# Six temporary tiles, a later load of the rope factors and later tails of products in a four-layer hybrid block

## The chip, the cores and the metric

The kernel runs on one core of one Trainium2 chip. The metric is the device time of one execution in microseconds (us). Before the change the median of three runs is 2697.6 us (2693.47 to 2699.81).

## The reference

A sequence of 1024 tokens (1024 wide) gets 16 learned tokens ahead of it, 1040 in all, and passes four layers. Each adds a branch of its normalised input to the residual:

```python
for i in range(DEPTH):
    kind = i % N_MIXERS
    j = i // N_MIXERS
    u = rmsnorm(h, norm_gain[i])
    if kind == 0:
        y = attention_branch(u, a_w_in[j], a_q_gain[j], a_k_gain[j], a_sinks[j], a_w_out[j], valid, pos)
    elif kind == 1:
        y = mlstm_branch(u, b_w_in[j], b_conv_w[j], b_conv_b[j], b_gate_bias[j], b_h_gain[j], b_w_out[j], valid)
    else:
        y = hgrn2_branch(u, c_w_in[j], lower_bounds[i], c_o_gain[j], c_w_out[j], valid)
    h = h + jnp.where(valid[None, :, None], y.astype(h.dtype), 0.0).astype(h.dtype)
```

Layers 1 and 4 are sliding-window attention: q and k are projected, normalised per head by their mean square, rotated (rope), and used in blocks of 128. Layer 2 is an mLSTM. Layer 3 is HGRN2, a linear recurrence with a decay for each key channel:

```python
q, k, v, z = _split(u @ w_in, (A_W, A_KVW, A_KVW, A_W))
q = rope(rmsnorm(q.reshape(bsz, lp, A_HEADS, A_HD), q_gain), pos)
k = rope(rmsnorm(k.reshape(bsz, lp, A_KV, A_HD), k_gain), pos)
...
o = o_inter + jnp.einsum('bhts,bhse->bhte', att, v_)
S_new = jnp.exp(A_last)[..., None] * S + jnp.einsum('bhsd,bhse->bhde', k_ * jnp.exp(A_last[:, :, None] - A), v_)
```

## The kernel before, in words

Everything is held transposed, channels on partitions and tokens along the free dimension, in three chunks of tokens: 0 with 400, 1 with 384, 2 with 256 columns (the last layer's first chunk has 384). Each projection of 1024 inputs to 128 outputs (`proj`, lines 245 to 269) is, for one chunk, 24 matmuls (L262): eight pieces of the inputs, and for each three products of split operands (high by high, high by low, low by high). The weights come by DMA on SP's queue (L240, two halves of 256 KB each) and are split by ScalarE (ACT, L195) and VectorE (DVE, L196).

The order on TensorE (PE) is the program's own: the layers build lists of steps, each with an assumed cost in ns, and `weave`, `later` and `spread` merge them (lines 56 to 108). On ACT, DVE, GpSimd (POOL) and SP a scheduler sets the order from those steps when the program is built, and an order once set is fixed: an instruction that waits holds up what stands behind it on its engine.

**Temporary tiles.** `tmp()` (L139) gives one of TMPS = 5 buffers of 404 columns. They serve the squares of the norms, the normalised input before it is split, the sigmoids, and the q and k chunks. `vtile()` (L136) gives one of 10 tiles that otherwise hold blocks of v.

**A chunk of q or k** (`qk_proj`, L515 to L546) goes like this. `evac`, right behind the chunk's last matmul: the rope factors of its columns are loaded into the one buffer `cs` (L520), ACT copies the product out (L523, tile dst) and squares it (L524, tile sq), and four DMAs copy dst with its halves swapped into the tile rot (L527). `stat`, 2000 ns of steps later: a matmul on PE (L533) sums sq over the partitions of each head, and ACT makes the reciprocal root of it (L361, L362). `rope`, 4000 ns after the chunk: DVE multiplies by the factors (L538 dst, L539 rot), adds (L540) and multiplies by the root (L541). At 6000 ns the chunk is split into high and low parts (`q_split` L492 and L493, `k_split` L473 to L476), and only then dst is free. Three tiles of a chunk are temporaries, except for the first k projection, which has rows of its own. There are 60 such chunks, 30 in layer 1 and 30 in layer 4. By the addresses in the built program, five buffers come to this in a run of q chunks: the Square of a chunk takes the buffer that dst of the chunk two before it held, and rot takes that of rot of the chunk before.

**The norm** (`Norm`, L371 to L425): the squares of eight pieces of x (L377) are summed by DVE (L381) in the tile of the first square, a matmul with ones sums over partitions (L389), and the tile then holds the factor until the eight `unit`s of the chunk have used it (L415).

**Layer 3** (`layer_c`, L1006 to L1283): for each of 8 heads the tokens are worked on in five regions (16, then four of 256). For a region, DVE and ACT make eight tiles X (`level`, L1098), and PE multiplies them in a burst of small matmuls (L1127, L1137). `tail0` (L1144) masks and reduces these products on DVE (L1154, L1163), and POOL copies the result into the tile `att` (L1165). `tail1` transposes keys on PE (L1187). `tail2`, for each block of 128: att times v (L1202), the running state S times the queries (L1204), and the product for the next state (L1209), which DVE adds to S (L1214). S is handed on 64 times, from block to block. The tails of region r are woven with the levels and the burst of region r + 1, behind a step without work that counts as TAIL_LAG = 600 ns:

```python
mx += weave(main[r], last)
last = [[TAIL_LAG, lambda: None, None]] + tails[r]
```

Of the kernel before, what the change touches and what calls it, by code (L numbers as in the profile page):

```python
# [9 lines left out]
F32 = mybir.dt.float32  # L10
# [5 lines left out]
P = 128  # L16
# [18 lines left out]
C_W = 256  # L35
B_COLS = 96
LOOKAHEAD = 12000.0
TAIL_LAG = 600.0
PRIO = 40
ROWS, TMPS, RAWS, YS = 8, 5, 2, 3  # L40
XS = 14
GAP, BURST = 200.0, 1300.0
KT_LAG = 500.0
# [12 lines left out]
def weave(a, b):  # L56

    ta, tb = sum(x[0] for x in a) + 1e-9, sum(x[0] for x in b) + 1e-9
    out, i, j, ca, cb = [], 0, 0, 0.0, 0.0
    while i < len(a) or j < len(b):  # L60
        if j >= len(b) or (i < len(a) and ca / ta <= cb / tb):
            ca += a[i][0]
            out.append(a[i])
            i += 1
        else:
            cb += b[j][0]
            out.append(b[j])
            j += 1
    return out
# [42 lines left out]
def hybrid_kernel(ctx: ExitStack, tc: tile.TileContext, ins, out, layers=(0, 1, 2, 3)):  # L112
    nc = tc.nc
    v, s, g, pe, sp = nc.vector, nc.scalar, nc.gpsimd, nc.tensor, nc.sync
# [11 lines left out]
    def nm(x):  # L126
        ctr[0] += 1
        return f"{x}{ctr[0]}"
# [7 lines left out]
    def vtile():  # L136
        return rpool.tile([P, 258], F32, tag="v", name=nm("v"), bufs=10)

    def tmp():  # L139
        return tpool.tile([P, 404], F32, tag="t", name=nm("t"), bufs=TMPS)  # L140
# [10 lines left out]
    def psa():  # L151
        return psum("pa", 1)
# [92 lines left out]
    def proj(src, evac, chunks=CHUNKS):  # L245
        st = {}

        def pre():
            st["w"] = weights(src, "m")

        groups = []
        for n, (c0, cn) in enumerate(chunks):
            grp = []
            for part in range(4):
                def fn(n=n, c0=c0, cn=cn, part=part):
                    if part == 0:
                        st[n] = psj()
                    h, l = st["w"]
                    acc = st[n]
                    for k in (2 * part, 2 * part + 1):  # L260
                        for i, (a, b) in enumerate(((h, uh), (h, ul), (l, uh))):
                            pe.matmul(acc[:, :cn], a[:, k, :], b[:, k, c0 : c0 + cn],  # L262
                                      start=(k == 0 and i == 0), stop=(k == KT - 1 and i == 2))
                    if part == 3:
                        evac(acc, n, c0, cn)

                grp.append([6 * cn * MM, fn, pre if (n == 0 and part == 0) else None])
            groups.append(grp)
        return groups
# [90 lines left out]
    def rstd_from(acc, dst, cn, n):  # L360
        s.activation(dst[:, :cn], acc[:, :cn], AF.Ln, bias=eps, scale=1.0 / n)  # L361
        s.activation(dst[:, :cn], dst[:, :cn], AF.Exp, scale=-0.5)  # L362
# [8 lines left out]
    class Norm:  # L371
# [1 line left out]
            self.i, self.acc, self.ps = i, {}, {}  # L373

        def sq(self, m, n, c0, cn, size=KT):
            q = tmp()[:, :cn]
            s.activation(q, x[:, m, c0 : c0 + cn], AF.Square)  # L377
            if m % size == 0:
                self.acc[n] = q
            else:  # L380
                v.tensor_tensor(self.acc[n], self.acc[n], q, op=ALU.add)  # L381
# [63 lines left out]
    def layer_a(i, j, first, last, fin):  # L445
        win, wout = ins["a_win"][j], ins["a_wout"][j]
        chunks = LAST_CHUNKS if last else CHUNKS
        R = {}
# [66 lines left out]
        def qk_proj(src, gcol, work, fsplit, ch):  # L515
            late = {}

            def evac(acc, n, c0, cn):
                cos_sin = R["mix"].tile([P, 2, 400], F32, tag="cs", name=nm("cs"), bufs=1)
                sp.dma_start(cos_sin[:, :, :cn], ins["rope"][:, :, c0 : c0 + cn].rearrange("a p t -> p a t"))  # L520
                dst, sq, rot = work(n, c0, cn)
                late[n] = dst, sq, rot, cos_sin
                s.activation(dst, acc[:, :cn], AF.Identity, scale=R["cons"][:, gcol : gcol + 1])  # L523
                s.activation(sq, acc[:, :cn], AF.Square)  # L524
                for q in range(4):
                    o = q ^ 1
                    sp.dma_start(rot[32 * q : 32 * q + 32], dst[32 * o : 32 * o + 32])  # L527

            def finish(n, c0, cn):
                def stat():  # L530
                    dst, sq, rot, _ = late[n]
                    st = psa()
                    pe.matmul(st[:, :cn], R["masks"][:, 0:P], sq, start=True, stop=True)  # L533
                    rstd_from(st, sq, cn, 64)

                def rope():
                    dst, sq, rot, cos_sin = late[n]
                    v.tensor_tensor(dst, dst, cos_sin[:, 0, :cn], op=ALU.mult)  # L538
                    v.tensor_tensor(rot, rot, cos_sin[:, 1, :cn], op=ALU.mult)  # L539
                    v.tensor_tensor(dst, dst, rot, op=ALU.add)  # L540
                    v.tensor_tensor(dst, dst, sq, op=ALU.mult)  # L541

                return [(D_Q[0], [4 * cn * MM, stat, None]), (D_Q[1], [0.0, rope, None]),
                        (D_Q[2], fsplit(lambda: late[n][0], n, c0, cn))]

            return proj(src, evac, ch), [finish(n, *c) for n, c in enumerate(ch)]  # L546

        def tile_of(groups, events):
# [198 lines left out]
        for i in range(3, 12):  # L747
            for t in (2 * (i // 3), 2 * (i // 3) + 1):
                at = [id(z) for z in body]
                q, k = (at.index(id(z)) if id(z) in at else -1  # L750
                        for z in (order["q", t, i % 3], order["S", i // 3 - 1, i % 3]))
# [254 lines left out]
    def layer_c(i, j, fin):  # L1006
# [256 lines left out]
        for h in range(8):  # L1263
# [14 lines left out]
            for r in range(5):  # L1278
                mx += weave(main[r], last)
                last = [[TAIL_LAG, lambda: None, None]] + tails[r]  # L1280
            body += weave(mx, fill)
# [182 lines left out]
```

## Time and profile before

| | us |
|---|---|
| median of 3 runs | 2697.6 |
| the profiled execution | 2690.46 |
| its span, first to last instruction | 2688.7 |
| PE busy | 2590.5 |
| DVE busy | 1959.5 |
| ACT busy | 1693.4 |
| POOL busy | 370.1 |

By the times of the trace, layer 1 runs to about 536 us, layer 2 from there to about 1600, layer 3 to about 2200, and layer 4 to the end. In the profile's rows, "PE pa L533 <- ACT t L524: 37.3, 15, 4.8" reads: PE's matmul of line 533 waited for ACT's instruction of line 524, 37.3 us in total, 15 times, 4.8 us the longest. In a timeline a row is start, duration, engine, line, operation and tiles, and in brackets how long the engine had stood idle and for whom. PEclk is the clock that TensorE was granted, 1.00 being full. SPq is SP's queue, which only issues DMAs.

### The profile page before, as it was taken

To read this page: it belongs to the slowest core of one execution; us is meant where nothing else is said; L and a number is where in the kernel's file an instruction comes from. 1 tells how busy PE (TensorE), PEld (TensorE's weight loads), DVE (VectorE), ACT (ScalarE), POOL (GpSimd) and SP (SyncE) were. 2 spreads that over 40 slices of the span, in tenths; PEclk is the share of its full clock that TensorE was granted. 3 is DMA by queue.
4 is the path that set the end of the run, shared out by engine and by line. 5 is a ranking of instruction groups with operands and counts; after the bars stand their busy time and mean duration, and the time that the engine had idled before them with its cause. 6 is when DMAs were issued, how large, how long until landed. Compare 5 with 4: busy or idle time off the path is not lost.

```text
span 2688.7 us, 54502 instructions
## 1 busy us (share of the span) xinstructions
PE 2590.5 (96%) x20276; PEld 2492.4 (93%) x20276; DVE 1959.5 (73%) x5337; ACT 1693.4 (63%) x4339; POOL 370.1 (14%) x760
## 2 busy tenths in 40 slices
PE   6899999999999999999999999999999998998999
PEld 5898989999999999999999998999999898898999
DVE  7787687974646474747475688978878978886886
ACT  7776777565454545454545657877676857766772
POOL 0343243000000000000000000101000000541450
PEclk8999999999999999999999999999999999999999
DMA  4223111011111111111111111101111013212212
GB/s 148 84 59 96 52 58 46 21 65 56 40 56 40 56 40 56 40 56 40 56 40 53 51 34 33 34 33 34 41 33 39 31 45 107 69 53 88 73 36 75
DMA packets 89786, 145.66 MB, mean 54 GB/s; under 512 B 12448, under 2 KB 42272, under 8 KB 89520
## 3 DMA queue, kind: packets, MB, share of 16 engines
q1 hardware_dynamic: 89520, 142.17, 16.9%
q8 instruction: 160, 2.62, 0.4%
q14 instruction: 106, 0.87, 0.1%
HBM read 127.28 MB, written 4.26 MB: 49 GB/s over the span
## 4 chain that ended last, share of the span: by engine, by line
PE 72%; DVE 12%; ACT 8%; issue 3%; POOL 2%; DMA 2%; SPq 0%; ACTq 0%; DVEq 0%; POOLq 0%
PE pj L262 35%; PE pj L345 14%; PE pj L307 9%; ACT Sm L633 1%; PE po L667 1%; PE pt L648 1%; PE po L890 1%; POOL Sm L637 1%; PE pa L904 1%; PE po L892 1%; DVE t L415 1%; DVE ul L196 1%; DVE Sm L630 1%; DVE x L348 1%; PE pj L303 1%
## 5 line engine op out<-in xcount | busy, mean ns | idle before, releaser
L262 PE MATMUL pj<-uh,wh 128*128 128x256 f32 (+2 forms) x2688 | 930.5, 346 | 3.4 <-ACT uh L195 3.4
L262 PE MATMUL pj<-ul,wh 128*128 128x256 f32 (+2 forms) x2688 | 871.7, 324 | 3.2 <-DVE ul L196 3.1
L262 PE MATMUL pj<-uh,wl 128*128 128x256 f32 (+2 forms) x2688 | 869.6, 324 | 0.0
L262 PEld LDWEIGHTS pj<-uh,wh 128*128 128x128 f32 x2688 | 513.4, 191 | 24.3 <-issue 6.4
L262 PEld LDWEIGHTS pj<-ul,wh 128*128 128x128 f32 x2688 | 513.7, 191 | 15.2 <-DVE ul L196 5.3
L262 PEld LDWEIGHTS pj<-uh,wl 128*128 128x128 f32 x2688 | 513.2, 191 | 0.1
L637 POOL TENSOR_SCALAR Sm<-Sm,s 128x256 f32<-128x256 f32 (+2 forms) x272 | 254.5, 947 | 410.7 <-DVE s L635 406.0
L196 DVE TENSOR_TENSOR wl<-wr,wh 128x512 fp32r<-128x512 f32 x336 | 228.7, 690 | 54.1 <-ACT wh L195 51.8
L195 ACT CAST wh<-wr 128x512 fp32r<-128x512 f32 x336 | 201.9, 616 | 97.9 <-PE pj L345 27.1
L348 DVE TENSOR_TENSOR x<-x,pj 128x384 f32<-128x384 f32 (+2 forms) x480 | 234.7, 510 | 38.8 <-PE pj L345 37.1
L345 PE MATMUL pj<-yh,wh 128*128 128x384 f32 (+2 forms) x768 | 252.9, 329 | 0.0
L345 PE MATMUL pj<-yl,wh 128*128 128x384 f32 (+2 forms) x768 | 248.0, 323 | 3.3 <-DVE yl L196 3.3
L345 PE MATMUL pj<-yh,wl 128*128 128x384 f32 (+2 forms) x768 | 246.6, 321 | 0.0
L307 PE MATMUL pj<-wh,uh 128*128 128x256 f32 x768 | 231.0, 301 | 0.0
L307 PE MATMUL pj<-wh,ul 128*128 128x256 f32 x768 | 216.4, 282 | 0.0
L307 PE MATMUL pj<-wl,uh 128*128 128x256 f32 x768 | 216.1, 281 | 0.0
L633 ACT ACTIVATE Sm<-Sm,s 128x257 f32<-128x257 f32 (+2 forms) x272 | 130.6, 482 | 84.6 <-DVE s L630 75.5
L432 DVE SCALAR_TENSOR_TENSOR t<-pj,t 128x384 f32<-128x384 f32 (+2 forms) x192 | 99.0, 515 | 107.0 <-ACT t L431 106.5
L433 ACT ACTIVATE t<-t 128x384 f32<-128x384 f32 (+2 forms) x240 | 117.8, 491 | 80.1 <-DVE t L432 79.0
L345 PEld LDWEIGHTS pj<-yl,wh 128*128 128x128 f32 x768 | 145.1, 189 | 5.7 <-DVE yl L196 5.2
L195 ACT CAST yh<-r 128x384 fp32r<-128x384 f32 (+2 forms) x120 | 57.3, 479 | 143.8 <-PE pj L345 126.2
L345 PEld LDWEIGHTS pj<-yh,wh 128*128 128x128 f32 x768 | 145.3, 189 | 1.7 <-DVE S L1214 0.3
(235 smaller groups left out, 5470.9 us busy)
## 6 DMA issues: line engine op xcount, KB each, us to landing
wr<-in_b_win SPq DMA_DIRECT2D x128, 256.0 KB, 2.9
wr<-in_a_win SPq DMA_DIRECT2D x80, 256.0 KB, 2.9
wr<-in_c_win SPq DMA_DIRECT2D x64, 256.0 KB, 2.8
cs<-in_rope SPq DMA_DIRECT2D x28, 384.0 KB, 3.3
wr<-in_a_wout SPq DMA_DIRECT2D x32, 256.0 KB, 2.7
wr<-in_b_wout SPq DMA_DIRECT2D x32, 256.0 KB, 2.7
cs<-in_rope SPq DMA_DIRECT2D x20, 256.0 KB, 2.7
t<-t SPq DMA_DIRECT2D x104, 48.0 KB, 2.2
```

What stands on the lines that cost most here:

```text
L195: s.copy(h, src)
L196: v.tensor_tensor(l, src, h.bitcast(F32), op=ALU.subtract)
L262: pe.matmul(acc[:, :cn], a[:, k, :], b[:, k, c0 : c0 + cn], start=(k == 0 and i == 0), stop=(k == KT - 1 and i == 2))
L303: pe.matmul(acc[:48, :256], um[0][:, k, :], m[:, kk, :], start=(k == 0 and m is wh), stop=(k == KT - 1 and m is wl))
L307: pe.matmul(acc[:cn, :256], a[:, k, c0 : c0 + cn], m[:, kk, :], start=(k == 0 and i == 0), stop=(k == KT - 1 and i == 2))
L345: pe.matmul(acc[:, :cn], a[:, k, mc], b, start=(k == 0 and i == 0), stop=(k == 1 and i == 2))
L348: v.tensor_tensor(x[:, m, c0 : c0 + cn], x[:, m, c0 : c0 + cn], acc[:, :cn], op=ALU.add)
L415: v.scalar_tensor_tensor(u, x[:, k, cs], ngain[:, self.i, k : k + 1], self.acc[n], op0=ALU.mult, op1=ALU.mult)
L432: v.scalar_tensor_tensor(a[:, :cn], z, 0.0, a[:, :cn], op0=ALU.min, op1=ALU.subtract)
L433: s.activation(a[:, :cn], a[:, :cn], AF.Exp)
L633: s.activation(Sm[:nq, u, : nk + 1], Sm[:nq, u, : nk + 1], AF.Exp, scale=-1.0, bias=st[:nq, u : u + 1], accum_out=den[:nq, u : u + 1])
L637: g.tensor_scalar(Sm[:nq, u, :nk], Sm[:nq, u, :nk], den[:nq, u : u + 1], None, op0=ALU.mult)
```

## The change

Four things change. TMPS is 6. The first square of a norm sum goes to a tile of the v pool where the chunk is chunk 2, so that this sum holds no temporary; its arithmetic is the same. The load of the rope factors moves from `evac` to `stat`, 2000 ns of steps later, and so behind the four rot DMAs of the same chunk in the program's text. TAIL_LAG is 2000. No instruction is added or taken away; PE's order changes only in layer 3.

```diff
-TAIL_LAG = 600.0
+TAIL_LAG = 2000.0
...
-ROWS, TMPS, RAWS, YS = 8, 5, 2, 3
+ROWS, TMPS, RAWS, YS = 8, 6, 2, 3
...
         def sq(self, m, n, c0, cn, size=KT):
-            q = tmp()[:, :cn]
+            q = (vtile() if n == 2 and m % size == 0 else tmp())[:, :cn]
             s.activation(q, x[:, m, c0 : c0 + cn], AF.Square)
...
             def evac(acc, n, c0, cn):
-                cos_sin = R["mix"].tile([P, 2, 400], F32, tag="cs", name=nm("cs"), bufs=1)
-                sp.dma_start(cos_sin[:, :, :cn], ins["rope"][:, :, c0 : c0 + cn].rearrange("a p t -> p a t"))
                 dst, sq, rot = work(n, c0, cn)
-                late[n] = dst, sq, rot, cos_sin
+                late[n] = dst, sq, rot
...
                 def stat():
-                    dst, sq, rot, _ = late[n]
+                    dst, sq, rot = late[n]
+                    cos_sin = R["mix"].tile([P, 2, 400], F32, tag="cs", name=nm("cs"), bufs=1)
+                    sp.dma_start(cos_sin[:, :, :cn], ins["rope"][:, :, c0 : c0 + cn].rearrange("a p t -> p a t"))
+                    late[n] = dst, sq, rot, cos_sin
```

In the changed program the lines between 521 and 527 stand two earlier (evac is L521 and L522, the rot DMAs L525), the load of the factors is L531, and the lines from 533 on stand one later. By its addresses, six buffers are two sets of three in a run of q chunks: the Square takes the buffer that the Square of the chunk two before it held (last used by the final product of its rope), dst that of rot, and rot that of dst.

**SP's queue, layer 1, the last five chunks of q and k ahead of the second pair's attention (253 to 272 us in the trace of before).** cs is the load of rope factors, `t<-t` a chunk's rot DMAs, wr a weight load. Before:

```order
L520 DMA cs_3084<-in_rope 128x2x256
L527 DMA t_3088<-t_3086 32x256 x4
L240 DMA wr_3437<-in_a_win 128x512
L520 DMA cs_3158<-in_rope 128x2x400
L527 DMA t_3162<-t_3160 32x400 x4
L240 DMA wr_3690<-in_a_win 128x512
L240 DMA wr_3694<-in_a_win 128x512
L520 DMA cs_3214<-in_rope 128x2x384
L527 DMA t_3218<-t_3216 32x384 x4
L520 DMA cs_3254<-in_rope 128x2x256
L527 DMA t_3258<-t_3256 32x256 x4
```

Now, for the same chunks:

```order
L531 DMA cs_3140<-in_rope 128x2x256
L240 DMA wr_3433<-in_a_win 128x512
L525 DMA t_3084<-t_3082 32x256 x4
L240 DMA wr_3437<-in_a_win 128x512
L525 DMA t_3160<-t_3158 32x400 x4
L531 DMA cs_3202<-in_rope 128x2x400
L525 DMA t_3216<-t_3214 32x384 x4
L531 DMA cs_3261<-in_rope 128x2x384
L240 DMA wr_3690<-in_a_win 128x512
L240 DMA wr_3694<-in_a_win 128x512
L531 DMA cs_3306<-in_rope 128x2x256
L525 DMA t_3254<-t_3252 32x256 x4
```

For the 400 and the 384 column chunks the rot DMAs now stand ahead of the chunk's own factors; for the two of 256 the factors still stand first.

**ACT, the last of these chunks (256 columns of k; 267 to 271 us in the trace).** Its copy out (L523) and its Square (L524), with the split of an earlier chunk (L473 to L476) around them. Before:

```order
L523 ACTIVATE t_3256<-pj_3225,cons_194 128x256
L474 CAST r_3279<-t_3160 64x400
L476 CAST r_3280<-r_3280 64x400
L473 CAST r_3281<-t_3160 64x400
L474 CAST r_3281<-t_3160 64x400
L524 ACTIVATE t_3257<-pj_3225 128x256
```

Now:

```order
L362 ACTIVATE t_3215<-t_3215 128x384
L521 ACTIVATE t_3252<-pj_3223,cons_194 128x256
L522 ACTIVATE t_3253<-pj_3223 128x256
L473 CAST r_3277<-t_3158 64x400
L474 CAST r_3277<-t_3158 64x400
```

The Square stood behind the split of the chunk two before it, whose tile it took; it now stands right behind the copy, ahead of that split.

**PE, layer 3, first head, third region (1680 to 1686 us in the trace).** po is the output that tail2 adds up, pa the product for the next state, pm the burst, pj a projection. Before:

```order
L1202 MATMUL po_19376<-att_18665,v_18868 128x128
L1204 MATMUL po_19376<-X_19617,S_19597 128x128
L1209 MATMUL pa_19714<-v_18868,kT_19681 128x128
L262 MATMUL pj_19673<-uh,wh_19440 128x400
L262 MATMUL pj_19673<-ul,wh_19440 128x400
L262 MATMUL pj_19673<-uh,wl_19441 128x400
```

Now:

```order
L262 MATMUL pj_19658<-uh,wl_19447 128x400
L1203 MATMUL po_19376<-att_18665,v_18868 128x128
L1205 MATMUL po_19376<-X_19617,S_19603 128x128
L1210 MATMUL pa_19792<-v_18868,kT_19705 128x128
L1203 MATMUL po_19796<-att_18665,v_18952 128x128
L1205 MATMUL po_19796<-X_19617,S_19794 128x128
L1210 MATMUL pa_19799<-v_18952,kT_19705 128x128
```

Before, six rows of projection, the burst of the next region and six more rows stood between the two blocks of the region. Now the burst stands ahead of both (right behind tail1), and the second block follows the first at once.

## The prediction

> **What bounds the kernel now.** First the page's table of engines and the view of the cores, to see which engine sets the time.
>
> ```profile
> PE 2590.5 (96%) x20276; PEld 2492.4 (93%) x20276; DVE 1959.5 (73%) x5337; ACT 1693.4 (63%) x4339; POOL 370.1 (14%) x760
> core 0: 2688.7 us, clock 0.986
> ```
>
> PE is busy 2590.5 of 2688.7 us. No matmul is added or taken away, so two things can be won: the 2688.7 − 2590.5 = 98.2 us in which PE stands, and the time lost at a lower clock, about 0.014 × 2688.7 = 38 us. Next, where these lie: busy time by layer (start and end, length; PE, PEld, DVE, ACT, POOL with their counts; granted clock, DMA share, GB/s).
>
> ```profile
> 78.00:536.00 458.00, 432.42 (x2825) 414.74 (x2824) 366.79 (x992) 315.40 (x845) 155.56 (x298) 0.98 0.19 57
> 536.00:1600.00 1064.00, 1059.87 (x6973) 1028.61 (x6973) 652.98 (x1647) 561.31 (x1313) 7.68 (x67) 1.00 0.15 48
> 1600.00:2200.00 600.00, 583.30 (x7211) 557.53 (x7210) 500.28 (x1600) 435.61 (x1227) 56.55 (x133) 0.99 0.12 38
> 2200.00:2689.00 489.00, 459.59 (x3018) 444.80 (x3016) 381.87 (x985) 323.42 (x835) 148.56 (x253) 0.98 0.23 69
> ```
>
> Layer 2 is full (4 us idle, clock 1.00): nothing can come from there. The attention layers have 25.6 and 29.4 us idle, layer 3 has 16.7. Third, the view of the waits, which says for whom (total, count, longest).
>
> ```profile
> PE pa L533 <- ACT t L524: 37.3, 15, 4.8
> PE po L1202 <- POOL att L1165: 16.0, 10, 3.5
> PE pa L389 <- DVE t L381: 7.4, 3, 4.0
> PE pt L648 <- POOL Sm L637: 7.3, 14, 1.2
> PE pa L533 <- ACT r L524: 2.1, 1, 2.1
> DVE S L1214 <- PE pa L1209: 15.1, 12, 2.8
> ```
>
> The statistics matmul waits for the Square (L524): 37.3 + 2.1 = 39.4 us, two fifths of all idle time. The attention part of layer 3 waits 16.0 us for `att`. The change touches both.
>
> **Why the Square is late.** SP's and DVE's timelines around 265 us, the place of the longest such wait.
>
> ```profile
> 253.21 0.38 SPq L520 DMA_DIRECT2D cs<-in_rope  x1
> 259.34 0.38 SPq L520 DMA_DIRECT2D cs<-in_rope  x1
> 265.90 0.38 SPq L520 DMA_DIRECT2D cs<-in_rope  x1
> 271.62 0.39 SPq L520 DMA_DIRECT2D cs<-in_rope  x1
> ...
> 258.89 0.42 DVE L539 TENSOR_TENSOR t<-t,cs 128x256 f32<-128x256 f32 x1
> 265.31 0.57 DVE L539 TENSOR_TENSOR t<-t,cs 128x400 f32<-128x400 f32 x1
> 266.51 0.57 DVE L541 TENSOR_TENSOR t<-t,t 128x400 f32<-128x400 f32 x1
> 269.56 0.57 DVE L475 TENSOR_TENSOR r<-t,r 64x400 fp32r<-64x400 f32 x1 [1.31 <-ACT r L473]
> ```
>
> Then ACT's and PE's timelines of the chunk behind.
>
> ```profile
> 267.56 0.47 ACT L523 ACTIVATE t<-pj,cons 128x256 f32<-128x256 f32 x1
> 270.21 0.38 ACT L524 ACTIVATE t<-pj 128x256 f32<-128x256 f32 x1
> 270.65 1.22 PE L533 MATMUL pa<-t,masks 128*128 128x256 f32 x2 [4.77 <-ACT t L524]
> ```
>
> Two things follow one another here. The loads of the factors come 6.13, 6.56 and 5.72 us apart: each starts when the rope before has read the one buffer (258.89 + 0.42, then 259.34; 265.31 + 0.57, then 265.90), and the rot DMAs of its chunk stand behind it on SP. So load, rot and rope form a loop. And the copy out ended at 268.03, but the Square began at 270.21, when the split of the chunk two before (L475, from 269.56) had let go of its tile. PE waited 4.77 us.
>
> **Square waits (term 1).** With six buffers the Square needs only the final product (L541) of the chunk two before: here 266.51 + 0.57 = 267.08. The copy, which by the old rule took the tile that this same product frees (it began at 267.56), needs only L539 of the chunk two before, 265.88, and so stands no longer in the way. The Square moves from 270.21 to 267.08, and 3.1 of the 4.77 us go. The first and last of the eleven long waits (39.4 us with five short ones):
>
> ```profile
> 79.10 0.57 DVE L541 TENSOR_TENSOR t<-t,t 128x400 f32<-128x400 f32 x1
> 81.82 0.38 ACT L524 ACTIVATE t<-pj 128x256 f32<-128x256 f32 x1 [0.69 <-DVE qs L493]
> 82.26 1.22 PE L533 MATMUL pa<-t,masks 128*128 128x256 f32 x2 [3.90 <-ACT t L524]
> ...
> 2538.95 0.56 DVE L541 TENSOR_TENSOR t<-t,t 128x384 f32<-128x384 f32 x1
> 2544.67 1.11 PE L533 MATMUL pa<-t,masks 128*128 128x256 f32 x2 [2.42 <-ACT t L524]
> ```
>
> At 82.26 the Square moves from 81.82 to 79.67, so 2.1 of 3.90 us go; at 2544.67 the product ended at 2539.51, long before PE came, and all of 2.42 goes. Done so for the eleven, with the ropes as late as now, it gives 2.1, 2.2, 1.7, 3.1, 3.8, 0, 2.0, 1.6, 2.3, 3.1 and 2.4, together 24.3. That is the low end; the high end is 39.4. The ropes themselves come sooner where loads follow closely, because the rot DMAs no longer stand behind the load.
>
> ```profile
> DMA to landing us min/median/max: 2.6/3.2/4.5
> ```
>
> The loop is then the load alone and two multiplications: 3.2 + 0.57 + 0.57 = 4.3 us, with hand-overs perhaps 4.7 (estimate), against some 6.1 now. PE needs 24 rows of projection for a chunk, by the chain of waits
>
> ```profile
> 644.96 18.46 PE pj L262 x120
> ```
>
> 18.46 / 120 = 0.154 us each, so 3.7 us: the loop stays the slower of the two, but by 1 us a chunk, not 2.4. I take **30**, two fifths of the way from 24.3 to 39.4. On ACT the splits that stood ahead of the Square now stand behind it; their readers are the attention blocks of the pair, and none of the large waits above is for them.
>
> **Clock behind the waits (term 2).** By the windows, the attention layers lose 0.02 × 458 = 9.2 and 0.02 × 489 = 9.8 us to the clock, and layer 3 loses 0.01 × 600 = 6 (rounding: ±0.005). Where it is lost, two windows and a wait:
>
> ```profile
> 271.00:275.00 4.00, 4.00 (x13) 3.78 (x13) 2.81 (x6) 2.92 (x7) 0.00 (x0) 0.50 0.32 90
> ...
> 1690.95 0.49 PE L1202 MATMUL po<-att,v 128*128 128x128 f32 x2 [2.28 <-POOL att L1165]
> 1691.00:1695.00 4.00, 4.00 (x62) 3.56 (x64) 2.22 (x12) 1.48 (x7) 0.00 (x0) 0.57 0.06 13
> ```
>
> After the wait of 4.77 us PE runs 4 us at half speed; after one of 2.28 us it does so too (0.57). So a wait must be shortened to below 2.28 us at the least to win this back. Of 19 in the attention layers, 30/39.4 is 14.5; as some waits are left near that, I take **12** (8 to 17).
>
> [...]
>
> **Norm sum (term 3).** Chunk 2's sum held one of the five buffers through a chunk of units.
>
> ```profile
> 44.05 1.22 PE L389 MATMUL pa<-t,const 128*128 128x256 f32 x2 [4.05 <-DVE t L381]
> ```
>
> This wait, 4.05 us, is of that chunk. Its squares can start earlier, but the eight sums on DVE still follow one another: 0 to 5, I take **2**. The v tile it takes costs nothing: ten stand there, and at these places the v blocks of the layer are not yet made.
>
> **Layer 3 (term 4).** A step of 2000 ns in place of 600 puts PE work between a region's burst and its tail2. Counted in rows of PE's order times 0.154 us, that distance is 4.9 to 13.4 us before and 9.6 to 19.7 now. The wait for `att` is 3.5 us at the longest, so I take **15** of 16.0 (12 to 16), and **5** of the clock's 6 (3 to 6).
>
> **The new cost (term 5).** What was spread between the blocks of a tail now stands ahead of them, so blocks follow each other more closely, and S is handed on from one to the next: L1209, then DVE's L1214, then the next block. Of the 64 hand-overs, 8 had at most 12 rows of projection between them, and none under 6. Now 4 have none, 15 have six, 11 have nine to thirteen. The shortest and longest hand-over of before:
>
> ```profile
> 2046.43 0.39 PE L1209 MATMUL pa<-v,kT 128*128 128x128 f32 x2
> 2046.85 0.35 DVE L1214 SCALAR_TENSOR_TENSOR S<-S,s,pa 128x128 f32<-128x128 f32 x1
> ...
> 2088.30 0.39 PE L1209 MATMUL pa<-v,kT 128*128 128x128 f32 x2
> 2091.64 0.33 DVE L1214 SCALAR_TENSOR_TENSOR S<-S,s,pa 128x128 f32<-128x128 f32 x1
> ```
>
> They take 0.77 and 3.67 us. Cover is att times v of the next block (0.49 us, row at 1690.95) and the rows, six being 0.92. At 0.77 only the four bare ones wait: 4 × 0.28 = 1 us. Midway, at 2.2 us, 4 × 1.7 + 15 × 0.8 = 19. In the first region, where tail1 now stands right ahead of tail2, PE waits about 1 us more for the transposed keys (estimate, from the same hand-over). I take **−6** of 2 to 20: the quoted short pair is of the close kind, and the long one comes where DVE had other work queued ahead and PE plenty to do.
>
> **Mixers (term 6).** Attention blocks wait 7.3 us for POOL (L648). With the projections done sooner POOL has less head start: 0 to 7 more, I take **−4**.
>
> **Sum.** 30 + 12 + 2 + 15 + 5 − 6 − 4 = 54, against the profiled execution's 2690.46: 2636.5. The median of the runs is 7.1 above that execution, so the forecast is **2643.6**.
>
> **Rivals.**
>
> A, *the later load makes the rope later.* Where the buffer is already free, the load now starts up to 2000 ns of steps later, and the Square waits for L541 of the chunk two before. With ropes 1 us later, each of the eleven gains shrinks by 1: 24.3 becomes 14, the clock gives 6. For it: the landing takes 3.2 us, not hidden if it starts with the statistics. Against: at the places that wait now the loads are held by the buffer, not by the program. 14 + 6 + 2 + 15 + 5 − 6 − 4 = 32: 2658.5, as median 2665.6. Chance 0.17.
>
> B, *hand-overs of S eat layer 3's gain.* Term 5 at its end of 20, and gaps that keep the clock low: 30 + 12 + 2 + 15 − 20 − 4 = 35, median 2662.6. For it: DVE is busy 500 of 600 us there. Chance 0.12.
>
> [...] Chance 0.03.
>
> D, *slower:* DVE stands queued at every close hand-over, each taking the longest 3.67 us. Waits: 4 × 3.2 + 15 × 2.3 + 11 × 1.3 = 61; behind 19 of them 4 us at 0.57, a loss of 1.7 each, 33. Against 30 + 12 + 2 + 15 − 4 = 55 won that is +39: median 2736.6. It decides from a cost of 55, or 1.8 us at each of 30. DVE's L1214 waited for PE in 12 cases and 15.1 us, so DVE is often the one that stands ready; that speaks against. Chance 0.05.
>
> E, *the change moves waits only:* the Square is free, but ACT or the rot DMAs are next, and PE reaches the end as late as now. Nothing is won beyond 0.2%, about 5.4 us, which is what a measurement of this kernel can tell from no change. Against: at 267.08 all that the Square needs is ready. Chance 0.05.
>
> **How the numbers follow.** The forecast has 0.58. All low ends together would be 24 + 8 + 0 + 12 + 3 − 20 − 7 = 20 won (median 2677.6), all high ends 39 + 17 + 5 + 16 + 6 − 2 = 81 (2616.6); neither meets wholly. 2618 to 2676 holds the forecast, A, B and C, and leaves out D, E and the corners. Faster: 0.58 + 0.17 + 0.12 + 0.03 = 0.90; same 0.05; slower 0.05.
>
> **What would show it.** Right: the row of PE waiting for ACT's Square falls from 39 to about 10 us, that for `att` to near nothing; the attention windows show clock 0.99 or 1.00; layer 2 still takes 1064 us; in layer 3 a new wait of PE for L1215's S of a few us. Loads of the factors in close runs come under 5 us apart. Wrong: Square waits of over 20 us (A), waits for S of over 15 us (B, D), or a new long wait on the path in the attention heads (E).

## The result, and the profile after

The changed kernel takes 2652.9 us (median of 4 runs, 2651.9 to 2654.3) against 2698.0 us before (4 runs, 2693.5 to 2699.8). The ratio is 0.9836, with a 95% interval of 0.9819 to 0.9853: 45 us faster. The forecast was 2643.6, 54 us faster, with a range of 2618 to 2676. The profiled execution took 2653.2 us; its span is 37.6 us shorter than that of before. The other 8 us are scatter: the execution profiled before lay some 7.6 us below its median, the one profiled after lies on it.

The page's table of engines and the view of the cores, after:

```profile
PE 2579.2 (97%) x20276; PEld 2481.9 (94%) x20276; DVE 1956.4 (74%) x5337; ACT 1691.1 (64%) x4339; POOL 367.6 (14%) x760
core 0: 2651.1 us, clock 0.992
```

PE's idle time fell from 98.2 to 2651.1 − 2579.2 = 71.9 us, that is by 26.3; its busy time fell by 11.3 for the same 20276 matmuls, and most of that is the clock: by the trace's own records of the granted clock, PE was busy at half clock for 66.1 us before and for 40.0 us after, and half of the difference is 13.0. Together 26.3 and 11.3 are the 37.6.

By layer, with the ends of the stretches moved by as much as the same instructions have moved there:

```profile
77.00:523.00 446.00, 431.13 (x2833) 412.43 (x2833) 369.10 (x998) 316.78 (x851) 155.16 (x297) 0.99 0.20 60
523.00:1586.00 1063.00, 1058.88 (x6984) 1028.12 (x6983) 653.51 (x1648) 563.12 (x1317) 8.06 (x68) 1.00 0.15 48
1586.00:2176.00 590.00, 579.29 (x7211) 556.27 (x7210) 497.55 (x1599) 434.66 (x1227) 55.99 (x133) 0.99 0.12 39
2176.00:2651.00 475.00, 455.22 (x3016) 439.25 (x3015) 382.32 (x984) 323.08 (x834) 146.64 (x253) 0.99 0.24 71
```

Layer 2 stays as it was (1063 us for 1064). Layer 1 takes 12 us less, layer 3 takes 10 and layer 4 takes 14. In the view of PE's waits (total, count, longest) the two large rows have shrunk, and four rows have come or grown (dots stand for rows left out):

```profile
PE pa L534 <- ACT t L522: 12.2, 10, 2.9
...
PE pj L345 <- DVE yl L196: 8.2, 9, 2.8
PE pt L649 <- POOL Sm L638: 7.2, 11, 1.6
PE po L1205 <- DVE S L1215: 5.5, 11, 1.4
...
PE pa L389 <- DVE t L381: 3.5, 2, 3.1
...
PE pm L1138 <- DVE X L1115: 2.5, 1, 2.5
PE pa L389 <- DVE v L381: 2.3, 1, 2.3
PE pa L1210 <- ACT kT L1190: 1.3, 1, 1.3
...
PE po L1203 <- POOL att L1166: 0.6, 1, 0.6
...
PE pa L534 <- ACT r L522: 0.4, 1, 0.4
```

The Square (12.2 + 0.4) costs 12.6 us where it cost 39.4, `att` 0.6 where it cost 16.0. New are the waits for S, for one tile X and for the transposed keys, 9.3 us together, and the output projection's wait for `yl`, which was 3.3 us, is now 8.2. Rows of one kernel scatter between executions: in a second execution of the changed kernel (the mark among the experiments) the Square's two rows are 14.5 + 0.4.

At the place shown before, the loads of the rope factors and the rot DMAs on SP, then the chunk behind on ACT and PE, now read:

```profile
253.57 0.53 SPq L531 DMA_DIRECT2D cs<-in_rope  x1
254.96 2.41 SPq L525 DMA_DIRECT2D t<-t  x4
258.05 0.38 SPq L531 DMA_DIRECT2D cs<-in_rope  x1
263.16 0.38 SPq L531 DMA_DIRECT2D cs<-in_rope  x1
```

```profile
259.14 0.47 ACT L521 ACTIVATE t<-pj,cons 128x256 f32<-128x256 f32 x1 [1.08 <-DVE t L541]
260.23 0.38 ACT L522 ACTIVATE t<-pj 128x256 f32<-128x256 f32 x1 [0.61 <-DVE t L542]
260.51 0.51 ACT L473 CAST r<-t 64x400 fp32r<-64x400 f32 x1
260.66 0.70 PE L534 MATMUL pa<-t,masks 128*128 128x256 f32 x2 [1.87 <-ACT t L522]
```

The loads are 4.5 and 5.1 us apart instead of about 6. The Square follows the copy, waits for the final product of the rope two chunks before (L542), and the split (L473) comes behind it, as the prediction had it. PE waits 1.87 us here where it waited 4.77.

### The profile page after: what moved, and what is told of

Read it like the earlier page. It is cut to its first block, busy times and chain, and to the rows that moved or that the text cites. A ratio compares the mean times of both kernels' runs of the same rounds, so it can differ in the third digit from the quotient of the medians.

```text
span 2651.1 us, 54471 instructions
## 1 busy us (share of the span) xinstructions
PE 2579.2 (97%) x20276; PEld 2481.9 (94%) x20276; DVE 1956.4 (74%) x5337; ACT 1691.1 (64%) x4339; POOL 367.6 (14%) x760
## 5 line engine op out<-in xcount | busy, mean ns | idle before, releaser
L348 DVE TENSOR_TENSOR x<-x,pj 128x384 f32<-128x384 f32 (+2 forms) x480 | 235.1, 511 | 36.4 <-PE pj L345 34.7
```

Source lines behind the costliest of these rows:

```text
L348: v.tensor_tensor(x[:, m, c0 : c0 + cn], x[:, m, c0 : c0 + cn], acc[:, :cn], op=ALU.add)
```

## The experiments

All were timed in 5 rounds against the kernel before, in three groups, each on one chip. Where kernels of different groups are compared, their ratios to the kernel before are used; an interval of such a ratio is about ±0.0014, or ±4 us.

**One part undone.** The changed kernel with five temporaries again:

```diff
-ROWS, TMPS, RAWS, YS = 8, 6, 2, 3
+ROWS, TMPS, RAWS, YS = 8, 5, 2, 3
```

> The changed kernel with TMPS back at 5. Theory (the tile count frees the Square, the later load only shortens the loop of load, rot and rope): the Square again waits for the split of the chunk two before, PE's wait for ACT's Square goes from 12.6 us to 25 to 35, and with the clock behind it the time rises by 20 to 30 us, to 2673 to 2683. Rival (the later load does most of it, since a rope that comes sooner also brings the split sooner): waits below 20 us, time up by 5 to 10, to 2658 to 2663.

Measured: 2685.3 us, 0.9969 of the kernel before [0.9957, 0.9980].

```profile
PE pa L534 <- ACT t L522: 38.4, 14, 4.8
PE pj L345 <- DVE yl L196: 3.3, 6, 0.8
```

The wait for the Square is back in full, although the load still stands in its later place. The time is 35 us above the changed kernel by the ratios, where the theory had 20 to 30: more hangs on the tile than it said. And the wait for `yl` is back at the 3.3 us of before: the two exchange.

With the load back in `evac`:

```diff
             def evac(acc, n, c0, cn):
+                cos_sin = R["mix"].tile([P, 2, 400], F32, tag="cs", name=nm("cs"), bufs=1)
+                sp.dma_start(cos_sin[:, :, :cn], ins["rope"][:, :, c0 : c0 + cn].rearrange("a p t -> p a t"))
                 dst, sq, rot = work(n, c0, cn)
```

> The changed kernel with the load of the rope factors back in evac, ahead of the rot DMAs. Theory: loads in close runs are again about 6 us apart instead of 4.5 to 5.5, ropes later, the Square waits for the final product of the chunk two before at some places: 18 to 25 us of Square waits in place of 12.6, time up by 8 to 14 us, to 2661 to 2667. Rival (six tiles alone decide): waits as in the changed kernel, time within 4 us of 2653. Second rival (the load's place decides): waits above 30, time up by 20 or more.

Measured: 2649.3 us, 0.9833 [0.9819, 0.9846], the same as the changed kernel or a little better; Square waits 10.5 us. The theory fell, and its first rival (six tiles alone decide) holds. SP's queue at the same place:

```profile
250.79 0.53 SPq L520 DMA_DIRECT2D cs<-in_rope  x1
251.37 3.93 SPq L527 DMA_DIRECT2D t<-t  x5
255.61 0.38 SPq L520 DMA_DIRECT2D cs<-in_rope  x1
260.77 0.38 SPq L520 DMA_DIRECT2D cs<-in_rope  x1
```

Loads 4.8 and 5.2 us apart with the load in its old place. So the later load did not shorten the loop; the tile did. The other half of the proof is SP's queue in the kernel with the later load and five buffers:

```profile
254.05 0.38 SPq L531 DMA_DIRECT2D cs<-in_rope  x1
254.65 2.74 SPq L525 DMA_DIRECT2D t<-t  x4
259.63 0.39 SPq L531 DMA_DIRECT2D cs<-in_rope  x1
```

These loads are 5.6 us apart again, the next ones 9.7 and 5.9. With five buffers the tile `rot` was that of the chunk before, and its DMAs had to wait for the same rope as the load. With six it is another, whose DMAs can run ahead of the rope. DVE's waits for these DMAs, in the kernel before and then in this one:

```profile
DVE t L538 <- DMA t<-t: 12.0, 13, 2.0
```

```profile
DVE t L538 <- DMA t<-t: 8.5, 10, 1.8
DVE t L538 <- DMA cs<-in_rope: 4.6, 6, 1.5
```

Before, the ropes waited for the rot DMAs and never for the load. Now they wait for both (in the changed kernel 5.0 us for rot and 10.2 for the load), so the rot DMAs no longer always come last, but they have not left the loop altogether.

Two more kernels, each with one part undone. With TAIL_LAG back at 600:

```diff
-TAIL_LAG = 2000.0
+TAIL_LAG = 600.0
```

> The changed kernel with TAIL_LAG back at 600. Theory: the waits for att come back (15 us), those for S, kT and the X tile go (9 us), and the clock behind the long ones is lost again (3 to 5 us): time up by 8 to 12 us, to 2661 to 2665. Rival (hand-overs of S and the like have eaten the gain): within 3 us of 2653.

Measured: 2658.1 us, 0.9869 [0.9856, 0.9883].

```profile
PE po L1203 <- POOL att L1166: 15.9, 11, 3.3
```

The wait for `att` is back, those for S, kT and the X tile are gone from the view. By the ratios (0.9869 against 0.9836 and 0.9838) the later tails are worth 8 to 9 us here, at the lower end of the 8 to 12 expected; against the kernel that follows below, which is of the same group, it is 6.5 us. That kernel has the norm sum back in a temporary:

```diff
-            q = (vtile() if n == 2 and m % size == 0 else tmp())[:, :cn]
+            q = tmp()[:, :cn]
```

> The changed kernel with the norm sum of chunk 2 back in one of the six temporaries. Theory: only the statistics of the first layer's chunk 2 come later, time up by 1 to 3 us, to 2654 to 2656. Rival (the held tile takes away the sixth buffer where q and k chunks run beside the norm, in the first chunks of layers 1 and 4): Square waits there come back, time up by 5 to 10, to 2658 to 2663.

Measured: 2651.6 us, 0.9842 [0.9829, 0.9856]: no difference that can be told. The rival that the held tile brings Square waits back is excluded by its 11.1 us. Nor did the 1 to 3 us that the theory had for the norm sum show.

**One or two parts alone.** The changed kernel again as the mark, and the kernel before with TMPS = 6 and nothing else:

> The changed kernel itself once more, as the mark for the three kernels beside it on the same chip: 0.983 to 0.984 of the kernel before.

Measured: 2651.7 us, 0.9838 [0.9824, 0.9851].

```diff
-ROWS, TMPS, RAWS, YS = 8, 5, 2, 3
+ROWS, TMPS, RAWS, YS = 8, 6, 2, 3
```

> The kernel before with TMPS = 6 and nothing else. Theory (formed after the four kernels that undo one part: the sixth tile alone frees the Square, and it shortens the loop of load, rot and rope too, because rot no longer waits for the rope of the chunk before; the load's new place does nothing): Square waits of 10 to 14 us, waits for att of 16 as before, and a time 5 to 9 us above the changed kernel, 36 to 41 below the kernel before. Rival (the tile works only together with the later load): Square waits above 18 us and less than 30 us won.

Measured: 2660.3 us, 0.9872 [0.9858, 0.9885], so 35 us of the 44 that the changed kernel won beside it, just under the 36 to 41 expected.

```profile
PE po L1202 <- POOL att L1165: 16.5, 10, 3.5
PE pa L533 <- ACT t L524: 10.6, 9, 4.0
...
PE pj L345 <- DVE yl L196: 8.2, 9, 2.7
```

The tile does this without any help: the Square's wait falls to 10.6, and the wait for `yl` rises to 8.2. Then both lines, TMPS = 6 and TAIL_LAG = 2000, without the two edits in the code:

> The kernel before with TMPS = 6 and TAIL_LAG = 2000, the other two edits left out. Theory (sixth tile some 35 us, later tails some 8, the load's place and the norm sum nothing): the changed kernel's time within 3 us, 0.983 to 0.984 of the kernel before, with 10 to 14 us of Square waits. Rival (the two small edits are worth something together): 4 us or more above the changed kernel.

Measured: 2648.4 us, 0.9821 [0.9807, 0.9834]. The changed kernel's time is reached with two numbers. Whether the other two edits cost the 4 us between 0.9821 and 0.9838 can't be told, as the intervals overlap; that they bring anything is not seen.

**Layer 3: what the later tails cost.** TAIL_LAG between the two:

```diff
-TAIL_LAG = 2000.0
+TAIL_LAG = 1300.0
```

> The changed kernel with TAIL_LAG = 1300. At 600 the waits for att are 16 us and those for S, kT and the X tile near none; at 2000 they are 0.6 and 9. Of the 64 hand-overs of S, 24 lie close here against 32 at 2000 and 8 at 600. Theory (both costs grow smoothly and weigh alike): waits for att of 3 to 6 us, the others 4 to 7, time within 3 us of the changed kernel. Rival (close hand-overs are what is left of layer 3's loss): 4 to 7 us faster than the changed kernel. Second rival (att decides): 4 to 7 us slower.

Measured: 2660.6 us, 0.9872 [0.9857, 0.9886], 9 us above the mark.

```profile
PE po L1205 <- DVE S L1215: 8.1, 8, 1.5
...
PE po L1203 <- POOL att L1166: 4.6, 6, 2.1
```

Both waits are there at once: 12.7 us, more than at 2000 (5.5 + 0.6), so the two costs do not simply pass into each other. In PE's order of this trace six hand-overs have no projection row between them, against four at 2000 and none at 600, and these six wait 6.5 of the 8.1 us. Of the 9 us, 6.6 are in these rows, and 2.4 were won back at the X tile and the keys; the rest (other waits and PE's busy time, 2580.7 us against 2575.1 of the mark) was not pinned down. The theory (within 3 us) fell; the second rival is nearest in size, but `att` is the smaller part of the wait, so its cause is not shown.

Then the two blocks of a region's tail2 moved apart, in the kernel of the two lines:

```diff
                 for b in range(len(REGIONS[r])):
+                    if b:
+                        ts.append([1000.0, lambda: None, None])
                     ts.append(S(640, tail2, r, b))
```

> The kernel of the two edits, with a step without work of 1000 ns between the two blocks of a region's tail2, so that projections come between them: the closest hand-over of S in PE's order has 2.34 us of work in place of 0.23, and 31 fewer are close. Theory (in layer 3 the hand-overs ate a part of what the later tails won): PE's waits for S fall from 5.5 to 6 us to below 1.5, those for att stay below 3, time 3 to 6 us below the kernel of the two edits. Rival (the projections that go between the blocks are then lacking ahead of them): waits for att or for the X tile come back, time within 2 us.

Measured: 2647.3 us, 0.9820 [0.9807, 0.9834], against 2648.4 for the same without the step.

```profile
PE po L1202 <- POOL att L1165: 6.4, 6, 1.7
...
PE pa L1209 <- ACT kT L1189: 1.9, 4, 0.6
...
PE pm L1137 <- DVE X L1114: 1.4, 3, 0.6
```

No row of PE waiting for S is left, but `att` waits 6.4 us: the rival holds. The projections that hide one hand-over are taken from the other; that layer 3 has no more of this filling is the likely reading, not a tested one.

**Where the Square's gain went.** Of 26.8 us won at the Square, 4.9 came back as a longer wait for `yl`. The largest case, on DVE and PE of the changed kernel:

```profile
2517.78 0.41 DVE L542 TENSOR_TENSOR t<-t,t 128x256 f32<-128x256 f32 x1
2518.10 0.55 DVE L196 TENSOR_TENSOR yl<-r,yh 128x384 fp32r<-128x384 f32 x1
```

```profile
2518.70 0.45 PE L345 MATMUL pj<-yl,wh 128*128 128x384 f32 x1 [2.75 <-DVE yl L196]
```

Before, PE waited 2.42 us for the Square of this chunk (row at 2544.67) and then found `yl` done. Now it does not wait there, comes sooner, and `yl` stands on DVE behind the rope's last product. The windows of some 14 us ahead of it, after and then before, show why nothing gives way (length, then PE, PEld, DVE, ACT and POOL busy with their counts, granted clock, DMA share, GB/s):

```profile
2505.00:2519.00 14.00, 11.08 (x70) 10.09 (x69) 13.59 (x39) 9.69 (x28) 5.93 (x12) 1.00 0.16 49
```

```profile
2542.50:2556.50 14.00, 11.83 (x65) 11.32 (x66) 11.94 (x34) 7.62 (x24) 5.16 (x9) 0.88 0.22 67
```

DVE is busy for 13.59 of 14 us, where it had 11.94. An attempt to set the splits ahead in its order:

```diff
-                return [0.0, fn, None]
+                return [0.0, hi(fn), None]
```

> The changed kernel with the splits of the output projection's inputs (yh, yl) at the high priority that the attention blocks have, so that on DVE they stand ahead of ropes and residual sums. Theory (PE, no longer held by the Square, comes to the output projection before DVE has got through its queue): PE's wait of 8.2 us for yl falls to 2 to 4 us, and the time falls by 3 to 6 us. Rival (DVE is full there, so what is put behind comes late instead): the wait goes to another row (ropes, Square, Sm or Pl), time within 2 us of the changed kernel.

Measured: 2654.3 us, 0.9849 [0.9836, 0.9863].

```profile
PE pa L534 <- ACT t L522: 16.6, 12, 3.1
...
PE pj L345 <- DVE x L348: 6.5, 6, 1.4
...
PE pj L345 <- DVE yl L196: 0.3, 1, 0.3
```

The wait for `yl` is gone, and 6.5 us for the residual sum (L348, 0.9 in the changed kernel) stand in its place; the Square's 16.6 lies 2.1 above the mark's 14.5, which is within what two executions differ by (12.2 and 14.5 for the changed kernel). The time is 2.5 us above the mark, inside the intervals: the rival holds. The engine is full there; its order only chooses who waits.

**What is left of the Square's wait.** Two buffers for the rope factors, which needs room: YS, the number of tiles for the output projection's inputs, goes to 2. The mark beside it has YS = 2 alone. Both have the load in `evac`.

```diff
-ROWS, TMPS, RAWS, YS = 8, 6, 2, 3
+ROWS, TMPS, RAWS, YS = 8, 6, 2, 2
...
-                cos_sin = R["mix"].tile([P, 2, 400], F32, tag="cs", name=nm("cs"), bufs=1)
+                cos_sin = R["mix"].tile([P, 2, 400], F32, tag="cs", name=nm("cs"), bufs=2)
```

> The changed kernel with the load back in evac, two buffers for the rope factors, and YS = 2 to make room for the second. Theory (what is left of the Square waits, 10 to 14 us, comes from the one buffer: load, two multiplications, load): in close runs loads no longer follow the rope before, Square waits fall below 5 us, and the time by 4 to 8 us below the same kernel with one buffer (YS = 2, beside it). Rival (DVE is full in these stretches, so the ropes come no sooner): Square waits and time within 2 to 3 us.

> The mark for the kernel with two buffers of rope factors: the same with one, load in evac, YS = 2. With YS = 3 it took 2649. Expected within 3 us of that, if the output projection's splits do not need the third tile; 5 to 10 us more if they do.

Measured: 2675.2 us with two buffers, 0.9921 [0.9909, 0.9934]; 2685.3 with one, 0.9960 [0.9947, 0.9972]. PE's waits with two, then with one:

```profile
PE pj L345 <- DVE yl L196: 17.1, 39, 1.3
...
PE pa L533 <- ACT t L524: 3.8, 7, 1.1
```

```profile
PE pj L345 <- DVE yl L196: 18.0, 38, 2.0
PE pa L533 <- ACT t L524: 11.9, 10, 3.0
```

The second buffer takes the Square's wait from 11.9 to 3.8 us (DVE's waits for the load, 5.6 us, are gone, and those for the rot DMAs fall from 10.3 to 3.8) and the time down by 10 us, a little more than the 4 to 8 expected. So most of what was left came from the loop round the one buffer of factors, and not from DVE's rate, at least in this kernel. The room for it is the difficulty: the third `yh`, `yl` tile that paid for it is worth some 34 us, by the ratios, where 5 to 10 had been expected. Of these, 11.6 are in the row for `yl` (18.0 against 6.4); PE's busy time is 21.8 us longer (2598.4 against 2576.6) at a clock of 0.994 and 0.993, so busy time does not follow the clock alone. Why it grows was not pinned down.

## Why the prediction was right, and by how much it was off

The sum was 54 us; 45 came by the medians and 37.6 between the two profiled executions, which the terms are measured on. The direction and the main mechanism held. The tile alone wins 34 to 36 us, by the kernel without it and by the kernel with nothing else. Term by term:

- **Square, forecast 30, measured 39.4 − 12.6 = 26.8.** The release by the final product in place of the split is what the chip does (row at 260.23: 0.61 us for L542). The size is nearly right (the second execution gives 39.4 − 14.9 = 24.5, the low end), but a reason given for going above 24.3 is wrong: "the rot DMAs no longer stand behind the load". With the load in its old place the loop is just as short; the sixth tile, which gives `rot` a buffer of its own, shortens it. A smaller reading was wrong too: the copy needs not only the multiplication of rot two chunks before (L539) but the sum behind it (L540, in the changed kernel L541), for which it waits 1.08 us at 259.14. Nothing hangs on it, as the Square needs the final product anyway.
- **Clock, 12 + 5 forecast, 11.3 measured** by PE's busy time, 13.0 by the clock records. In this pair of executions it is the term that fell shortest; in the second execution of the changed kernel busy time fell by 15.4, so a good part of the miss is scatter. The step that failed is "a wait must be shortened to below 2.28 us at the least to win this back": the length of a wait did not decide alone (one of 2.75 us had no half clock behind it, one of 1.87 us had), as the last section shows.
- **Norm sum, 2 forecast, 7.4 − 5.8 = 1.6 measured** in the waits, and nothing in the time. Even the 1.6 is not this edit's: with six tiles and the sum in a temporary the wait for it is 6.4 us (norm edit alone undone) and 5.7 (sixth tile alone).
- **`att`, 15 forecast, 15.4 measured.** Without that edit the time is 8 to 9 us higher by the ratios, and between the kernel of one line and that of two lie 13 to 14 us; with ±4 us on each of these times both go with the net of 15 won and 9 lost and some clock.
- **Hand-overs, −6 forecast, −9.3 measured:** 5.5 for S and 1.3 for the keys, the two parts that were priced, and 2.5 for one tile X, which was not. Its burst now stands ahead of the blocks that used to delay it. The longest hand-over of before was 3.78 us and not the 3.67 that was quoted; nothing hangs on it.
- **Mixers, −4 forecast, 0 measured** (7.3 and 7.2). A price for PE coming sooner was due, but in another row: `yl`, −4.9, and −3.4 in small rows, which is what remains of the 37.6. The prediction had looked for it on POOL; DVE was the engine without slack.

26.8 + 11.3 + 1.6 + 15.4 − 9.3 + 0.1 − 4.9 − 3.4 = 37.6. The last term closes the sum by its making, so the sum is no proof of the others; the kernels above are.

Of the rivals, A shows in the ropes' waits for the load (10.2 us, with the load in its old place 4.6), but not in the time (0.9836 and 0.9833); the single buffer that it spoke of is what holds most of the rest, as the two buffers show. B's mechanism was there at half of its price (9.3 of 20). D did not come. E came in small: a tenth of the gain was paid again further on.

## What to carry to other kernels

Count which buffer each step frees, and for whom: one more tile broke two chains at once here, since both the next Square and the next copy DMA had waited for a buffer, while moving the load in the program changed nothing as long as its buffer decided when it could start. When a stall of the busiest engine is removed, look at each queue that had caught up during the stall, by its busy share in that stretch; what is full there will be the next to wait for. Spacing that hides one hand-over is taken from another, so sweep such a number with both waits in view, and try its values: 1300 took 0.9872 of the kernel before, 600 took 0.9869, which can't be told from it, and 2000 took 0.9838.

## What the hardware showed that was not expected

The length of a stall alone did not decide whether the granted clock fell behind it. The same wait for `yl` in two executions of the changed kernel, first the second execution (the mark among the experiments) and the window behind it:

```profile
2516.95 0.44 PE L345 MATMUL pj<-yl,wh 128*128 128x384 f32 x1 [2.74 <-DVE yl L196]
```

```profile
2518.10:2521.40 3.30, 3.30 (x13) 3.30 (x12) 3.21 (x10) 1.55 (x6) 0.94 (x3) 0.50 0.00 0
```

Half clock (0.50) for 3.3 us behind a wait of 2.74 us. In the first, after 2.75 us (row at 2518.70):

```profile
2518.70:2522.10 3.40, 3.34 (x21) 2.98 (x22) 3.25 (x9) 1.75 (x4) 2.10 (x4) 1.00 0.00 0
```

Full clock (1.00). By the clock records in the traces of the kernel before and of the changed kernel, half clock came in stretches of 3.413 us (12 before, 10 after) or 6.827 us (5 and 1), leaving out one that runs past the end of each span. In each of the two traces these stretches begin within 0.01 us of whole multiples of 3.4133 us from each other: before, the first begins at 15.55 us and the last at 2544.83, which is 741 times 3.4133 later. Cut into steps of that length from those points, the stalls differ. The Square's wait of 2.42 us in the kernel before (row at 2544.67) falls with 2.41 us into one step (2541.42 to 2544.83), and the next is at half clock; the 2.75 us in the first execution of the changed kernel lie across an edge at 2517.60, the steps hold 1.65 and 1.10 us of idle, and both that follow are at full clock. For the second execution, one step counted back from 2518.10, where its window at half clock begins, would hold some 2.3 of the 2.74 us (an estimate from its two rows above). Counted over the two traces, from where their clock records begin, for steps at full clock: with more than 1.85 us of idle PE, the next step was at half clock in each of 23 cases; with 0.98 to 1.85 us in 5 of 27; with less in none of 1471. In the changed kernel a stall of 1.87 us (row at 260.66) was followed by 3.41 us at half clock from 261.39 on, and the one of 2.75 us by none. What sets these points in time no trace here shows.

So the clock's loss differs between executions of one kernel: the two executions of the changed kernel had half clock for 41 and 31 us (mean granted clock 0.992 and 0.994). Their spans are only 0.5 us apart (2651.1 and 2650.6), as PE's idle time went the other way (71.9 and 75.5 us); the term of the clock could not be priced from one profile here.
